# RWKV solver in a hybrid encoder: single 128x1024 stream transposes, and a chain bank given to the attention

## The chip, the cores and the metric

One core of a Trainium2 chip. The metric is the device time of one execution in microseconds, the median of several runs. Engine names in the profile: PE is TensorE's matmuls, PEld its weight loads, DVE VectorE, ACT ScalarE, POOL GpSimd, SP SyncE.

## The reference

Two layers over x of 512 tokens by 1024 channels. Each layer computes

```
h  = RMSNorm(x);  P = h @ W_in
yA = bidirectional Mamba-2 SSD          (8 heads of 64)
yB = bidirectional RWKV-7 time mix      (8 heads of 64) * silu(gate)
yC = differential attention             (4 heads, two softmax maps each) * silu(gate)
yD = grouped-query attention            (4 query heads of 128, 2 key heads) * silu(gate)
x  = x + RMSNorm(concat(yA, yB, yC, yD) @ W_out)
```

The part that matters here is the RWKV scan, for each head and each direction a state S of 64x64 over 512 steps:

```
sa  = S a_t
S   = S * w_t + outer(sa, b_t) + outer(v_t, k_t)      a = -kk, b = kk * a
y_t = S r_t
```

## The kernel before

All is float32. The large projections split each weight and each activation into a high and a low float32r part and take three products; the low part of a weight is made on GpSimd from ScalarE's high part (L144, L145). A plain float32 product is two instructions on TensorE in the trace.

**RWKV.** `rwkv` goes over four pairs of heads, j = 0 to 3 (L522). The scan is done in eight chunks of 64 steps. For each pair, both heads (e), both directions (d) and all chunks (pairs cp, halves p) are worked at once: 32 blocks of 64x64. In a chunk, steps that depend on one another form a triangular system, and its inverse is needed. The solver (L537 to L599) inverts the 16x16 diagonal blocks on VectorE, 15 steps of two small operations each (L556 to L563), with the four blocks of a chunk along the partitions and the 32 systems side by side, and then builds the 64x64 inverse from them by three rounds of block products `ph` (L589 to L598).

To bring the diagonal blocks into that layout and back, the kernel uses VectorE's transposes of 32x32 blocks and ScalarE's copies:

- L548 to L551: four ScalarE copies of 32 partitions each gather the quarter blocks on the diagonal of `ba` (the tile AT0) into half of DT; one transpose of 128x512; one multiply-add under the mask `th` picks the right 16 columns into As2.
- L565 to L576: two scalings by `th` make Dx; a transpose of 128x512 and four copies fill DN (the inverse blocks); a second transpose and eight copies fill DT (their transposes). DN and DT were set to zero by GpSimd before.

Then follow the groups of 32 small products, each into two PSUM banks, one for each head e: `pm` (L582), `ph`, `px` (L604), `pu` (L611), `pw` (L616), `pq` (L621, L623), `pp` (L636), `py` (L647). In pm and px the output goes to `half[p ^ e]`: for the second head, the block of partitions 0 to 63 is written to 64 to 127, and the other way round. The copies of A (L466 to L469) and the reads in pu and pw follow that swap. `ph` writes to `half[p]`, without a swap. Last comes the chain over the chunks (L659 to L676): for each chunk and direction a product `bk` and one VectorE operation for the next state.

**PSUM.** Eight banks: two `pj` for projections, two `g` for all else in RWKV, one `ga` for the attention (scores, transposed probabilities `ptp`, outputs `ob`, transposed q and k `pqt`), and for the RWKV part `ch0`, `ch1` and `yb`. `G2` names the pair g, g, `C2` the pair ch0, ch1.

**The order of the work.** `fill` hands out pieces of the attention and of the projections between the solver's steps, as many microseconds' worth as constants such as F_SV, F_MG and F_CH say; `ahead` hands out the next pair's preparation. That makes the program's order. A planner then makes each engine's fixed order from it: the earliest in program order goes first, and what waits for a bank or a result may be passed by later work.

Of the kernel before, what the change touches and what calls it, by code (L numbers as in the profile page):

```python
# [10 lines left out]
F32 = mybir.dt.float32  # L11
F32R = mybir.dt.float32r
AF = mybir.ActivationFunctionType
ALU = mybir.AluOpType
# [40 lines left out]
C_TH = C_NOM + 64  # L55
C_I64 = C_TH + 2
C_N = C_I64 + 64

# [17 lines left out]
def trunk(ctx: ExitStack, tc: tile.TileContext, x_in, win, wwd, wdt, wout, w2a, cols, rows, sscal, consts, out, dbg=None,  # L76
# [4 lines left out]
    def mm(o, lhsT, rhs, start, stop, skip=False):  # L81
        PE.matmul(o, lhsT, rhs, start=start, stop=stop, skip_group_check=skip)  # L82
# [27 lines left out]
    id64 = cst[:, C_I64:C_I64 + 64]  # L110
    th = [cst[:, C_TH + n:C_TH + n + 1] for n in range(2)]
    nhalf = cst[:, C_NHALF:C_NHALF + 16]
# [140 lines left out]
    def rwkv(i, lay, pw, ps, rp, fill):  # L253
# [162 lines left out]
        half = [slice(0, 64), slice(64, 128)]  # L416
        quad = [(slice(32 * q, 32 * q + 32), slice(32 * (q % 2), 32 * (q % 2) + 32)) for q in range(4)]

# [5 lines left out]
        def banks(tags, shape, nm):  # L424
            return [ps.tile(shape, F32, tag=t, name=nm) for t in tags]

        G2, C2 = ("g", "g"), ("ch0", "ch1")
        zeros = cr[:, 272:273].to_broadcast([128, 128])
# [19 lines left out]
        def turned(src, nm):  # L448

            pt = ps.tile([128, 4, 128], F32, tag="g", name=nm)  # L450
            for cp in range(4):
                PE.transpose(pt[:, cp, :], src[:, cp * 128:cp * 128 + 128], ident)
            return pt.rearrange("p c (e k) -> p e c k", e=2)
# [3 lines left out]
        def by_tokens(j):  # L457

            s = sts[j]
            yield from products(j, 1)  # L460
            s["KT"], s["A"] = tokens("KT", "kt"), tokens("A", "ta")
            for d in range(2):
                S.activation(VT[:, :, d], turned(s["v"][d], "pv5"), AF.Copy)
                S.activation(s["KT"][:, :, d], turned(chans(s["BK"][d][:, 1]), "pk5"), AF.Copy)
                yield
                pt = turned(chans(s["a"][:, d]), "pa5")  # L466
                S.activation(s["A"][:, 0, d], pt[:, 0], AF.Copy)
                for p in range(2):
                    S.activation(s["A"][half[1 - p], 1, d], pt[half[p], 1], AF.Copy)  # L469
                yield  # L470
# [51 lines left out]
        for j in range(4):  # L522
# [13 lines left out]

            unit = lambda t, q: t[quad[q][0], :, :, :, quad[q][1]].rearrange("p e d c (h t) -> p t h (e d c)", h=2)  # L537
            thu = lambda t, q: t[quad[q][0]].rearrange("p (t h u) -> p t h u", t=16, h=2)
            sv = rp.tile([128, 1024], F32, tag="sv", name="sv", bufs=1)
            As = sv[:, 0:512].rearrange("p (t s) -> p t s", t=16)  # L540
            As2 = sv[:, 512:768].rearrange("p (t s) -> p t s", t=16)
            Ti = sv[:, 768:1024].rearrange("p (t s) -> p t s", t=16)
            DT, DN = tokens("DT", "dt"), tokens("DN", "dn")
            close = DT[:, 0].rearrange("p d c t -> p (d c t)")
            G.memset(DN, 0.0)
            G.memset(sv[:, 768:1024], 0.0)
            G.memset(sv[:, 768:1024:17], 1.0)
            for q in range(4):  # L548
                S.activation(thu(close, q), unit(ba, q), AF.Copy)
            V.transpose(out=sv[:, 0:512], in_=close)  # L550
            V.scalar_tensor_tensor(As2, As[:, :, 0:16], th[0], As[:, :, 16:32], op0=ALU.mult, op1=ALU.add)  # L551
            G.memset(DT, 0.0)

            bam = AT[0].rearrange("p e d c a t -> p (e d c) a t")[:, :, 0, :]
            G.tensor_tensor(bam, bam, nomask.unsqueeze(1).to_broadcast([128, 16, 64]), op=ALU.mult)
# [8 lines left out]

            Dx = sv[:, 0:512].rearrange("p (t h s) -> p t h s", t=16, h=2)  # L565
            for h in range(2):
                V.tensor_scalar(Dx[:, :, h, :], Ti, th[h], None, op0=ALU.mult)
            close = sv[:, 512:1024]
            V.transpose(out=close.rearrange("p (t h s) -> p t h s", t=16, h=2), in_=Dx.rearrange("p t h s -> p s h t"))
            for q in range(4):  # L570
                S.activation(unit(DN, q), thu(close, q), AF.Copy)
            V.transpose(out=close, in_=sv[:, 0:512])
            for q in range(4):
                for e in range(2):
                    S.activation(unit(DT, (q + 2 * e) % 4)[:, :, :, 8 * e:8 * e + 8], thu(close, q)[:, :, :, 8 * e:8 * e + 8],
                                 AF.Copy)  # L576
            step(1, F_MG)
# [3 lines left out]
            for d, cp, e, p in every:  # L581
                mm(pm[e][half[p ^ e], 4 * d + cp, :], ba[half[p], e, d, cp, :], DN[half[p], e, d, cp, :], True, True)  # L582
            S.activation(flat(Mp[:, 0]), pm[0], AF.Copy)
# [19 lines left out]
            for d, cp, e, p in every:  # L603
                mm(px[e][half[p ^ e], 4 * d + cp, :], ka[half[p], e, d, cp, :], VT[half[p], e, d, cp, :], True, True)  # L604
            S.activation(flat(X0[:, 0]), px[0], AF.Copy)
# [4 lines left out]
            for d, cp, e, p in every:  # L610
                mm(pu[e][half[p], 4 * d + cp, :], TT[half[p ^ e], e, d, cp, :], X0[half[p ^ e], e, d, cp, :], True, True)  # L611
            S.activation(flat(U0[:, 0]), pu[0], AF.Copy)
            V.tensor_copy(flat(U0[:, 1]), pu[1])
            pw = banks(G2, [128, 8, 64], "pw")
            for d, cp, e, p in every:
                mm(pw[e][half[p], 4 * d + cp, :], TT[half[p ^ e], e, d, cp, :], A[half[p ^ e], e, d, cp, :], True, True)  # L616
            step(1, F_MG)
# [6 lines left out]
            for p in range(2):  # L624
                V.tensor_tensor(Q[:, :, p::2], pq[p].rearrange("p (d c) v -> p d c v", d=2),
                                lamC[:, :, p::2].unsqueeze(3).to_broadcast([128, 2, 4, 64]), op=ALU.mult)
            W = tokens("W", "kt")
            S.activation(flat(W[:, 0]), pw[0], AF.Copy)
# [30 lines left out]
            for cc in range(1, 8):  # L659
                if cc == C_LAG:  # L660
                    ahead.finish()
                    if j < 3:
                        ahead.gens = [products(j + 1, 0)]
                Sn = [None, None]
                for d in range(2):
                    if cc < 7:
                        bk = ps.tile([128, 8, 64], F32, tag=f"ch{d}", name=f"bk{d}")
                        for e in range(2):
                            mm(bk[half[e], 0, :], P[half[e], d, cc, :], St[d][half[e]], True, True)
                        Sn[d] = rp.tile([128, 64], F32, tag=f"S{d}", name=f"S{d}", bufs=2)  # L670
                        V.scalar_tensor_tensor(Sn[d], bk[:, 0, :], lamC[:, d, cc:cc + 1], Q[:, d, cc, :],
                                               op0=ALU.mult, op1=ALU.add)
                    for e in range(2):
                        mm(yb[half[e], rev(d, cc)], St[d][half[e]], R[half[e], d, cc, ::1 - 2 * d], False, True, True)
                St = Sn
                step(2, F_CH)  # L676
# [241 lines left out]
    def pT_av(p, va, qb, ps, ap):  # L918

        pt = ps.tile([128, 4, 128], F32, tag="g", name="ptp")  # L920
        for kt in range(4):
            PE.transpose(pt[:, kt, :], p[:, kt * 128:kt * 128 + 128], ident)
        ptS = ap.tile([128, 4, 128], F32, tag="ptS", name="ptS", bufs=1)
        S.activation(ptS, pt, AF.Copy)
        ob = ps.tile([128, 128], F32, tag="g", name="ob")
        for kt in range(4):
            mm(ob, ptS[:, kt, :], va[:, kt, :], kt == 0, kt == 3)
        return ob
# [252 lines left out]
    ps = Bank(psc, {"pj": 2, "g": 2, "ga": 1})  # L1181
    pa = Bank(psc, ps.bufs, {"g": "ga"})
    hT["hi"] = hpool.tile([128, 8, L], F32R, tag="hhi", name="hhi")
# [9 lines left out]
    for i in range(depth):  # L1193
# [9 lines left out]
        with tc.tile_pool(name="psr", bufs=1, space=PSUM, reuse_waits="tile") as psr, \  # L1203
                tc.tile_pool(name="rw", bufs=1, reuse_waits="tile") as rp:
            rwkv(i, lay, pw, Bank(psc, ps.bufs, {}, Bank(psr, {"ch0": 1, "ch1": 1, "yb": 1})), rp, fill)

# [131 lines left out]
def _consts():  # L1338
# [11 lines left out]
    c[:, C_NOM:C_NOM + 64] = (s[:, None] // 16 < np.arange(64)[None, :] // 16)  # L1350
    for n in range(2):
        c[:, C_TH + n] = (p % 32 // 16 == n)
    c[:, C_I64:C_I64 + 64] = (s[:, None] == np.arange(64)[None, :])
# [104 lines left out]
```

## Time and profile before

| | us |
|---|---|
| median of 3 runs (1862.32 to 1870.21) | 1866.43 |
| the profiled execution | 1859.53 |
| its span, first to last instruction | 1857.7 |
| TensorE matmuls busy | 1600.4 (86%) |
| VectorE busy | 1031.5 (56%) |
| ScalarE busy | 937.2 (50%) |
| GpSimd busy | 694.7 (37%) |

The mean granted clock of TensorE is 0.927 of full speed. The span is what lies between the first and the last instruction; the execution's own time is a little longer. Busy time counts an engine's instructions without its waits; matmuls overlap, so their busy time is that of their union. A group's row gives the busy time, the mean of one in ns, and behind the second bar the idle time of the engine before it and what ended it.

### The profile page before, as it was taken

Reading aid. Unit: us, or ns where it says so; the run is one execution under the profiler, and the core shown is the slowest. Engines: PE = TensorE matmul, PEld = TensorE weight load, DVE = VectorE, ACT = ScalarE, POOL = GpSimd, SP = SyncE. Lnnn points to the kernel's source line nnn. Section 1 sums busy time; section 2 is a strip of 40 time slices with the busy share of each in tenths; the row PEclk is TensorE's granted clock in tenths of the full one; section 3 lists DMA queues with packets and bytes.
Section 4 is the critical chain, followed back from the end, with each engine's and each line's share of the span. In section 5 each row is a group of like instructions: output and inputs, shape, how many; then the busy total and the mean of one; then the engine's idle time right before and its main releaser. Section 6 shows DMA issues by size and latency. Waiting matters only on the chain. (4 is left out here: it accounts for less than half of the span.)

```text
span 1857.7 us, 36925 instructions
## 1 busy us (share of the span) xinstructions
PE 1600.4 (86%) x15200; PEld 1305.4 (70%) x15200; DVE 1031.5 (56%) x2098; ACT 937.2 (50%) x1750; POOL 694.7 (37%) x712
## 2 busy tenths in 40 slices
PE   6888987987888898988897999889689888999888
PEld 6567766766766777866785777676577666777666
DVE  4565465654573436886246554646455724378852
ACT  4657365457437245443346663744664472454431
POOL 4443233323152225444444333233332422355343
PEclk9889988989989899999999798989898898999999
DMA  4111101111011014222421010011110110141223
GB/s 151 61 40 39 36 26 44 44 35 41 25 35 52 30 41 147 70 70 91 136 99 51 33 42 30 29 48 43 35 46 19 35 52 25 52 138 57 91 82 117
DMA packets 57513, 108.50 MB, mean 58 GB/s; under 512 B 6784, under 2 KB 8704, under 8 KB 57344
## 3 DMA queue, kind: packets, MB, share of 16 engines
q1 hardware_dynamic: 57344, 106.14, 17.2%
q8 instruction: 119, 1.95, 0.4%
q14 instruction: 50, 0.41, 0.1%
HBM read 95.63 MB, written 10.49 MB: 57 GB/s over the span
## 5 line engine op out<-in xcount | busy, mean ns | idle before, releaser
L145 POOL TENSOR_TENSOR wlo<-wf,whi 128x512 fp32r<-128x512 f32 x228 | 316.9, 1396 | 510.2 <-ACT whi L144 475.6
L82 PE MATMUL pjt<-whi,hhi 128*128 128x256 f32 x960 | 297.0, 309 | 10.6 <-ACT raw L270 9.5
L82 PE MATMUL pjt<-wlo,hhi 128*128 128x256 f32 x960 | 290.9, 303 | 1.8 <-POOL wlo L145 1.8
L82 PE MATMUL pjt<-whi,hlo 128*128 128x256 f32 x960 | 288.7, 301 | 0.0
L144 ACT ACTIVATE whi<-wf 128x512 fp32r<-128x512 f32 x228 | 141.7, 629 | 199.6 <-PE pjt L82 91.5
L82 PEld LDWEIGHTS pjt<-whi,hhi 128*128 128x128 f32 x960 | 194.8, 203 | 26.7 <-ACT raw L270 10.6
L82 PEld LDWEIGHTS pjt<-whi,hlo 128*128 128x128 f32 x960 | 194.7, 203 | 9.1 <-issue 7.4
L82 PEld LDWEIGHTS pjt<-wlo,hhi 128*128 128x128 f32 x960 | 194.5, 203 | 9.0 <-issue 6.0
L82 PE MATMUL pjc<-hhi,whi 128*128 128x512 f32 x384 | 159.4, 416 | 9.3 <-ACT raw L270 5.2
L82 PE MATMUL pjc<-hlo,whi 128*128 128x512 f32 x384 | 157.1, 409 | 0.0
L82 PE MATMUL pjc<-hhi,wlo 128*128 128x512 f32 x384 | 156.4, 409 | 0.0
L900 ACT ACTIVATE p<-sc,nm 128x512 f32<-128x512 f32 x96 | 65.8, 685 | 124.9 <-DVE nm L897 113.4
L897 DVE TENSOR_REDUCE nm<-sc 128x1 f32<-128x512 f32 x96 | 65.9, 687 | 107.5 <-PE sc L82 106.6
L82 PE MATMUL sc<-qT,qT 64*128 64x512 f32 (+1 forms) x256 | 103.2, 502 | 20.5 <-DVE qT L938 7.2
L82 PE MATMUL mix<-whi,ylo 128*128 128x512 f32 x256 | 106.3, 415 | 5.4 <-DVE ylo L1241 5.4
L82 PE MATMUL mix<-wlo,yhi 128*128 128x512 f32 x256 | 104.4, 408 | 0.0
L82 PE MATMUL mix<-whi,yhi 128*128 128x512 f32 x256 | 99.6, 411 | 2.0 <-ACT yhi L1240 2.0
L82 PEld LDWEIGHTS pjc<-hhi,whi 128*128 128x128 f32 x384 | 75.7, 197 | 30.8 <-ACT raw L270 6.0
L82 PEld LDWEIGHTS pjc<-hhi,wlo 128*128 128x128 f32 x384 | 75.4, 196 | 19.5 <-issue 3.0
L1248 ACT ACTIVATE whi<-wf 128x512 fp32r<-128x512 f32 x64 | 40.5, 632 | 94.4 <-PE mix L82 59.4
L82 PEld LDWEIGHTS pjc<-hlo,whi 128*128 128x128 f32 x384 | 75.4, 196 | 16.7 <-issue 2.2
L1249 POOL TENSOR_TENSOR wlo<-wf,whi 128x512 fp32r<-128x512 f32 x32 | 44.4, 1391 | 105.8 <-ACT whi L1248 101.1
(349 smaller groups left out, 3681.4 us busy)
## 6 DMA issues: line engine op xcount, KB each, us to landing
wf<-in_win_dram SPq DMA_DIRECT2D x224, 256.0 KB, 3.0
wf<-in_wout_dram SPq DMA_DIRECT2D x64, 256.0 KB, 2.7
y<-y_dram SPq DMA_DIRECT2D x24, 256.0 KB, 3.3
xt<-in_x_dram SPq DMA_DIRECT2D x8, 512.0 KB, 4.3
y_dram<-y SPq DMA_DIRECT2D x16, 256.0 KB, 2.7
y_dram<-rs SPq DMA_DIRECT2D x8, 256.0 KB, 2.0
x_dram<-t SPq DMA_DIRECT2D x8, 256.0 KB, 2.3
xt<-x_dram SPq DMA_DIRECT2D x4, 512.0 KB, 3.8
```

What stands on the lines that cost most here:

```text
L82: PE.matmul(o, lhsT, rhs, start=start, stop=stop, skip_group_check=skip)
L144: S.activation(hi, wf, AF.Copy)
L145: G.tensor_tensor(lo, wf, hi.bitcast(F32), op=ALU.subtract)
L897: V.tensor_reduce(nm, sc, axis=AX, op=ALU.max, negate=True)
L900: S.activation(p, sc, AF.Exp, bias=nm, accum_out=sm)
L1248: S.activation(hi, wf, AF.Copy)
L1249: (V if kt % 2 else G).tensor_tensor(lo, wf, hi.bitcast(F32), op=ALU.subtract)
```

## The change

The transposes work on whole tiles of 128x1024 and carry the off-diagonal quarter blocks along; masks (`at`, seven columns of constants instead of two) pick what is wanted. The copies and the memsets of DN and DT are gone, and so is the swap of partition halves in A, pm, px, pu and pw. pw is issued behind pq. The attention's transposed probabilities and outputs use a bank `gb` during RWKV (in the rest of the layer `ga` as before); `C2` is now `ch` and one of the two g banks, and the chain's second direction uses g.

```diff
-    th = [cst[:, C_TH + n:C_TH + n + 1] for n in range(2)]
+    at = [cst[:, C_TH + n:C_TH + n + 1] for n in range(7)]
...
-        G2, C2 = ("g", "g"), ("ch0", "ch1")
+        G2, C2 = ("g", "g"), ("ch", "g")
...
-                pt = turned(chans(s["a"][:, d]), "pa5")
-                S.activation(s["A"][:, 0, d], pt[:, 0], AF.Copy)
-                for p in range(2):
-                    S.activation(s["A"][half[1 - p], 1, d], pt[half[p], 1], AF.Copy)
+                S.activation(s["A"][:, :, d], turned(chans(s["a"][:, d]), "pa5"), AF.Copy)
...
-            sv = rp.tile([128, 1024], F32, tag="sv", name="sv", bufs=1)
-            As = sv[:, 0:512].rearrange("p (t s) -> p t s", t=16)
+            sv = rp.tile([128, 1536], F32, tag="sv", name="sv", bufs=1)
+            As = sv[:, 0:1024].rearrange("p (t h s) -> p t h s", t=16, h=2)
...
-            G.memset(DN, 0.0)
...
-            for q in range(4):
-                S.activation(thu(close, q), unit(ba, q), AF.Copy)
-            V.transpose(out=sv[:, 0:512], in_=close)
-            V.scalar_tensor_tensor(As2, As[:, :, 0:16], th[0], As[:, :, 16:32], op0=ALU.mult, op1=ALU.add)
-            G.memset(DT, 0.0)
+            blocks = lambda t: t.rearrange("p u (q t) -> p t q u", q=4)
+            whole = lambda t: t.rearrange("p e d c t -> p (e d c) t")
...
+            V.transpose(out=sv[:, 0:1024].rearrange("p (t q u) -> p t q u", t=16, q=4), in_=blocks(bam))
+            V.scalar_tensor_tensor(As2, As[:, :, 0, 0:16], at[0], As[:, :, 0, 16:32], op0=ALU.mult, op1=ALU.add)
+            V.scalar_tensor_tensor(As2, As[:, :, 1, 0:16], at[1], As2, op0=ALU.mult, op1=ALU.add)
+            V.scalar_tensor_tensor(As2, As[:, :, 1, 16:32], at[2], As2, op0=ALU.mult, op1=ALU.add)
...
-            for h in range(2):
-                V.tensor_scalar(Dx[:, :, h, :], Ti, th[h], None, op0=ALU.mult)
-            close = sv[:, 512:1024]
-            V.transpose(out=close.rearrange("p (t h s) -> p t h s", t=16, h=2), in_=Dx.rearrange("p t h s -> p s h t"))
             for q in range(4):
-                S.activation(unit(DN, q), thu(close, q), AF.Copy)
-            V.transpose(out=close, in_=sv[:, 0:512])
-            for q in range(4):
-                for e in range(2):
-                    S.activation(unit(DT, (q + 2 * e) % 4)[:, :, :, 8 * e:8 * e + 8], thu(close, q)[:, :, :, 8 * e:8 * e + 8],
-                                 AF.Copy)
+                V.tensor_scalar(Dx[:, :, q, :], Ti, at[3 + q], None, op0=ALU.mult)
+            V.transpose(out=blocks(whole(DN)), in_=Dx.rearrange("p t q s -> p s q t"))
+            V.transpose(out=blocks(whole(DT)), in_=Dx)
...
-                mm(pm[e][half[p ^ e], 4 * d + cp, :], ba[half[p], e, d, cp, :], DN[half[p], e, d, cp, :], True, True)
+                mm(pm[e][half[p], 4 * d + cp, :], ba[half[p], e, d, cp, :], DN[half[p], e, d, cp, :], True, True)
...
-                        bk = ps.tile([128, 8, 64], F32, tag=f"ch{d}", name=f"bk{d}")
+                        bk = ps.tile([128, 8, 64], F32, tag="g" if d else "ch", name=f"bk{d}")
...
-        pt = ps.tile([128, 4, 128], F32, tag="g", name="ptp")
+        pt = ps.tile([128, 4, 128], F32, tag="h", name="ptp")
...
-        ob = ps.tile([128, 128], F32, tag="g", name="ob")
+        ob = ps.tile([128, 128], F32, tag="h", name="ob")
...
-            rwkv(i, lay, pw, Bank(psc, ps.bufs, {}, Bank(psr, {"ch0": 1, "ch1": 1, "yb": 1})), rp, fill)
+            pa.names["h"], pa.other = "gb", Bank(psr, {"gb": 1})
+            rwkv(i, lay, pw, Bank(psc, ps.bufs, {}, Bank(psr, {"ch": 1, "yb": 1})), rp, fill)
+            pa.names["h"] = "ga"
```

px loses its swap like pm, and pu and pw read `half[p]` of TT, X0 and A. The lines of pw stand behind the evacuation of pq into Q, ahead of the copies into W.

## Rows read from the trace of the kernel before

**Rows 1.** Stretches: length, busy PE, PEld, DVE, ACT, POOL, PEclk, DMA share, GB/s
```profile
110.00:680.00 570.00, 487.11 (x5987) 398.89 (x5988) 305.61 (x673) 306.03 (x572) 185.02 (x180) 0.92 0.11 36
1033.00:1604.00 571.00, 491.30 (x5991) 402.12 (x5991) 305.67 (x673) 306.52 (x574) 185.18 (x180) 0.91 0.11 36
...
420.70:427.30 6.60, 3.54 (x13) 2.94 (x14) 0.29 (x1) 6.41 (x13) 5.33 (x5) 0.50 0.17 59
```

**Rows 2.** TensorE's waits, stretch 110 to 680: total us, times, longest
```profile
PE ptp L922 <- DVE p L1057: 7.7, 7, 2.4
...
PE ptp L922 <- ACT p L900: 5.9, 5, 2.7
...
PE pv L82 <- ACT bh L284: 5.1, 2, 4.6
...
PE sc L82 <- ACT p L900: 2.6, 3, 1.1
...
PE pjt L82 <- ACT raw L270: 2.0, 1, 2.0
PE sc L82 <- ACT y L1059: 1.9, 2, 1.6
PE sc L82 <- ACT y L1080: 1.7, 1, 1.7
...
PE ptp L922 <- ACT KT L464: 1.4, 1, 1.4
...
PE pqt L933 <- ACT y L1059: 1.3, 1, 1.3
```

**Rows 3.** Groups of instructions: ScalarE's copies around the solver, both layers
```profile
L575 ACT ACTIVATE DT<-sv 32x256 f32<-32x256 f32 x64 | 41.8, 652 | 0.7
...
L571 ACT ACTIVATE DN<-sv 32x512 f32<-32x512 f32 x32 | 35.5, 1109 | 6.0 <-DVE sv L569 5.3
L549 ACT ACTIVATE DT<-AT 32x512 f32<-32x512 f32 x32 | 35.3, 1102 | 7.6 <-DVE AT L444 7.3
...
L469 ACT ACTIVATE A<-pa 64x256 f32<-64x256 f32 x32 | 12.1, 380 | 0.4
```

**Rows 4.** ScalarE in order of time, in the third solver: start, length
```profile
414.81 5.30 ACT L575 ACTIVATE DT<-sv 32x256 f32<-32x256 f32 x8
...
422.53 0.63 ACT L284 ACTIVATE bh<-sqc 128x512 fp32r<-128x512 f32 x1
```

**Rows 5.** Small products on TensorE: two runs in time, then groups
```profile
318.94 2.08 PE L82 MATMUL ph<-DN,Mp 64*64 64x64 f32 x64
...
324.48 1.16 PE L82 MATMUL px<-VT,AT 64*64 64x64 f32 x64
...
L82 PE MATMUL ph<-DN,Mp 64*64 64x64 f32 x1024 | 37.9, 227 | 12.9 <-DVE DN L597 12.9
...
L82 PE MATMUL pu<-X,DN 64*64 64x64 f32 x512 | 17.7, 261 | 8.5 <-DVE X L606 6.6 <-ACT X L605 1.9
...
L82 PE MATMUL pm<-DN,AT 64*64 64x64 f32 x512 | 16.5, 224 | 0.0
...
L82 PE MATMUL px<-VT,AT 64*64 64x64 f32 x512 | 13.5, 222 | 0.0
...
L82 PE MATMUL pw<-A,DN 64*64 64x64 f32 x512 | 12.9, 246 | 0.0
```

**Rows 6.** VectorE's groups around the solver; L551 by source line: min/median/max
```profile
L569 DVE STREAM_TRANSPOSE sv<-sv 128x512 f32<-128x512 f32 x8 | 8.9, 1111 | 0.1
...
L572 DVE STREAM_TRANSPOSE sv<-sv 128x512 f32<-128x512 f32 x8 | 5.7, 711 | 5.9 <-ACT DN L571 5.9
...
L551 DVE SCALAR_TENSOR_TENSOR sv<-sv,cst x8: 867/1988/2012, 116.2 to 1470.9; 128x256 f32<-128x256 f32 x8
```

**Rows 7.** VectorE's evacuations of pq and pp
```profile
L639 DVE TENSOR_TENSOR P<-pp,cst 128x256 f32<-128x256 f32 x32 | 13.3, 415 | 4.8 <-PE pp L82 4.3
...
L625 DVE TENSOR_TENSOR Q<-pq,lamC 128x512 f32<-128x512 f32 x16 | 10.3, 684 | 3.9 <-PE pq L82 3.9
```

More of the change, by code (lines that the diff above doesn't have):

```diff
@@ L55 @@
 C_TH = C_NOM + 64
-C_I64 = C_TH + 2
+C_I64 = C_TH + 7
 C_N = C_I64 + 64
@@ L416, in rwkv @@
         half = [slice(0, 64), slice(64, 128)]
-        quad = [(slice(32 * q, 32 * q + 32), slice(32 * (q % 2), 32 * (q % 2) + 32)) for q in range(4)]
         each = [(cp, e, p) for cp in range(4) for e in range(2) for p in range(2)]
@@ L534, in step @@
                 fill(us)
-            unit = lambda t, q: t[quad[q][0], :, :, :, quad[q][1]].rearrange("p e d c (h t) -> p t h (e d c)", h=2)
-            thu = lambda t, q: t[quad[q][0]].rearrange("p (t h u) -> p t h u", t=16, h=2)
-            sv = rp.tile([128, 1024], F32, tag="sv", name="sv", bufs=1)
-            As = sv[:, 0:512].rearrange("p (t s) -> p t s", t=16)
-            As2 = sv[:, 512:768].rearrange("p (t s) -> p t s", t=16)
-            Ti = sv[:, 768:1024].rearrange("p (t s) -> p t s", t=16)
-            DT, DN = tokens("DT", "dt"), tokens("DN", "dn")
-            close = DT[:, 0].rearrange("p d c t -> p (d c t)")
-            G.memset(DN, 0.0)
-            G.memset(sv[:, 768:1024], 0.0)
-            G.memset(sv[:, 768:1024:17], 1.0)
-            for q in range(4):
-                S.activation(thu(close, q), unit(ba, q), AF.Copy)
-            V.transpose(out=sv[:, 0:512], in_=close)
-            V.scalar_tensor_tensor(As2, As[:, :, 0:16], th[0], As[:, :, 16:32], op0=ALU.mult, op1=ALU.add)
-            G.memset(DT, 0.0)
+            sv = rp.tile([128, 1536], F32, tag="sv", name="sv", bufs=1)
+            As = sv[:, 0:1024].rearrange("p (t h s) -> p t h s", t=16, h=2)
+            As2 = sv[:, 1024:1280].rearrange("p (t s) -> p t s", t=16)
+            Ti = sv[:, 1280:1536].rearrange("p (t s) -> p t s", t=16)
+            DT, DN = tokens("DT", "dt"), tokens("DN", "dn")
+            G.memset(sv[:, 1280:1536], 0.0)
+            G.memset(sv[:, 1280:1536:17], 1.0)
+            blocks = lambda t: t.rearrange("p u (q t) -> p t q u", q=4)
+            whole = lambda t: t.rearrange("p e d c t -> p (e d c) t")
             bam = AT[0].rearrange("p e d c a t -> p (e d c) a t")[:, :, 0, :]
+            V.transpose(out=sv[:, 0:1024].rearrange("p (t q u) -> p t q u", t=16, q=4), in_=blocks(bam))
+            V.scalar_tensor_tensor(As2, As[:, :, 0, 0:16], at[0], As[:, :, 0, 16:32], op0=ALU.mult, op1=ALU.add)
+            V.scalar_tensor_tensor(As2, As[:, :, 1, 0:16], at[1], As2, op0=ALU.mult, op1=ALU.add)
+            V.scalar_tensor_tensor(As2, As[:, :, 1, 16:32], at[2], As2, op0=ALU.mult, op1=ALU.add)
             G.tensor_tensor(bam, bam, nomask.unsqueeze(1).to_broadcast([128, 16, 64]), op=ALU.mult)
@@ L563, in rwkv @@
                 V.tensor_tensor(Ti[:, jj + 1:16, 0:jj + 1], Ti[:, jj + 1:16, 0:jj + 1], o3, op=ALU.add)
-            Dx = sv[:, 0:512].rearrange("p (t h s) -> p t h s", t=16, h=2)
-            for h in range(2):
-                V.tensor_scalar(Dx[:, :, h, :], Ti, th[h], None, op0=ALU.mult)
-            close = sv[:, 512:1024]
-            V.transpose(out=close.rearrange("p (t h s) -> p t h s", t=16, h=2), in_=Dx.rearrange("p t h s -> p s h t"))
-            for q in range(4):
-                S.activation(unit(DN, q), thu(close, q), AF.Copy)
-            V.transpose(out=close, in_=sv[:, 0:512])
-            for q in range(4):
-                for e in range(2):
-                    S.activation(unit(DT, (q + 2 * e) % 4)[:, :, :, 8 * e:8 * e + 8], thu(close, q)[:, :, :, 8 * e:8 * e + 8],
-                                 AF.Copy)
+            Dx = sv[:, 0:1024].rearrange("p (t q s) -> p t q s", t=16, q=4)
+            for q in range(4):
+                V.tensor_scalar(Dx[:, :, q, :], Ti, at[3 + q], None, op0=ALU.mult)
+            V.transpose(out=blocks(whole(DN)), in_=Dx.rearrange("p t q s -> p s q t"))
+            V.transpose(out=blocks(whole(DT)), in_=Dx)
             step(1, F_MG)
@@ L603, in rwkv @@
             for d, cp, e, p in every:
-                mm(px[e][half[p ^ e], 4 * d + cp, :], ka[half[p], e, d, cp, :], VT[half[p], e, d, cp, :], True, True)
+                mm(px[e][half[p], 4 * d + cp, :], ka[half[p], e, d, cp, :], VT[half[p], e, d, cp, :], True, True)
             S.activation(flat(X0[:, 0]), px[0], AF.Copy)
@@ L610, in rwkv @@
             for d, cp, e, p in every:
-                mm(pu[e][half[p], 4 * d + cp, :], TT[half[p ^ e], e, d, cp, :], X0[half[p ^ e], e, d, cp, :], True, True)
+                mm(pu[e][half[p], 4 * d + cp, :], TT[half[p], e, d, cp, :], X0[half[p], e, d, cp, :], True, True)
             S.activation(flat(U0[:, 0]), pu[0], AF.Copy)
             V.tensor_copy(flat(U0[:, 1]), pu[1])
-            pw = banks(G2, [128, 8, 64], "pw")
-            for d, cp, e, p in every:
-                mm(pw[e][half[p], 4 * d + cp, :], TT[half[p ^ e], e, d, cp, :], A[half[p ^ e], e, d, cp, :], True, True)
             step(1, F_MG)
@@ L626, in rwkv @@
                                 lamC[:, :, p::2].unsqueeze(3).to_broadcast([128, 2, 4, 64]), op=ALU.mult)
+            pw = banks(G2, [128, 8, 64], "pw")
+            for d, cp, e, p in every:
+                mm(pw[e][half[p], 4 * d + cp, :], TT[half[p], e, d, cp, :], A[half[p], e, d, cp, :], True, True)
             W = tokens("W", "kt")
@@ L1181, in trunk @@
     ps = Bank(psc, {"pj": 2, "g": 2, "ga": 1})
-    pa = Bank(psc, ps.bufs, {"g": "ga"})
+    pa = Bank(psc, ps.bufs, {"g": "ga", "h": "ga"})
     hT["hi"] = hpool.tile([128, 8, L], F32R, tag="hhi", name="hhi")
@@ L1350, in _consts @@
     c[:, C_NOM:C_NOM + 64] = (s[:, None] // 16 < np.arange(64)[None, :] // 16)
-    for n in range(2):
-        c[:, C_TH + n] = (p % 32 // 16 == n)
+    b16 = s // 16
+    for n, m in enumerate((b16 % 2 == 0, b16 == 2, b16 >= 2, b16 == 0, b16 == 1, b16 == 2, b16 == 3)):
+        c[:, C_TH + n] = m
     c[:, C_I64:C_I64 + 64] = (s[:, None] == np.arange(64)[None, :])
```

## The prediction

> **What bounds the kernel now.** I read the table by stretches first, then TensorE's waits by cause, then the groups of instructions, then a few stretches in order of time. The two stretches in which the solver runs (the RWKV part of each layer) hold 1141 of the 1857.7 us. In each TensorE is busy 487 to 491 of some 570 us, while VectorE and ScalarE stand at 306 and GpSimd at 185 [rows 1]: TensorE sets the pace, and no other engine is near its own limit. It idles 82.9 us in the first and 79.7 in the second, 162.6 together, and it was granted 0.92 and 0.91 of its clock, so 45.6 + 51.4 = 97 us of full-speed work are lost beside: 0.6 us for each idle one. From within one wait of 4.6 us on, the granted clock was 0.50, the lower of the two levels, for 6.6 us [rows 1]. The change can gain in three ways: TensorE waits less, keeps the higher level more, or issues less. The list of waits shows that no single one rules: the kinds that bear on the change are 1.3 to 7.7 us a stretch each, and they end on VectorE and ScalarE in turn [rows 2]. The second layer's stretch is the first's over again (571 us, 491.3 busy), so I work with the first and double.
>
> **ScalarE's copies.** Each of the eight solvers loses 4 + 4 + 8 copies. They are 35.3 + 35.5 + 41.8 = 112.6 us in all [rows 3], 14 a solver. The copies of A go from three to one in each direction: two of 0.38 us, with a third of that width, become one twice as wide, between 0.38 and 0.76, so 6 to 12 us more. Two GpSimd memsets a solver go as well; GpSimd waits for others most of the time, and they count as nothing. ScalarE is not the bound, so its 120 us are not 120 us of the span. What counts are TensorE's waits for a ScalarE result that stood behind these copies. The clearest: eight copies into DT run for 5.30 us, and only behind them the norm's bh at 422.53 [rows 4]. TensorE waits 4.6 us for that bh (the longest of "pv from bh") [rows 2]. Of the waits of the transposed probabilities for p (5.9, the longest 2.7) I take 4.0: the longest and one of 1.3 lie in the fourth solver among its DN and DT copies. Of "raw" 2.0, of the wait behind KT 1.4, and of the scores waiting for p 1.1, its longest. That is 4.6 + 4.0 + 2.0 + 1.4 + 1.1 = 13.1 a layer, **26** in both. Bounds: 0, where the next late result stands right behind, and these rows in full in both layers, 34.
>
> The chain itself (copies, transpose, copies) also gets shorter, but the product that needs DN, pm, waited 0.0 [rows 5]: filler from the projections hides it, so I count nothing. If that cover were gone, the chain's 4 + 4 + 8 copies a solver would be worth up to 14 us each. The first half gains little in any case: four copies of 1.10, a transpose of 0.71 and one multiply-add of up to 1.99 are 7.1 us; in their place come a transpose of twice the size and three multiply-adds.
>
> **VectorE's added work.** A transpose of 128x512 takes 0.71 plain and 1.11 with a strided read [rows 6]. The three of 128x1024 have a strided read, a strided read and write, and a strided write. A strided write is not in the trace; I price it like the read and add 0.4 for each half: 2.2 + 3.0 + 2.2 = 7.4 against 2.5 before, so 4.9 more (bounds 1.7, all plain, and 6.5, all strided on both sides). Two more multiply-adds, 0.87 to 1.99 each; I take the low end, since one of the three meets GpSimd's masking as the one before did: 1.7. Two more scalings of 128x256, priced like P's evacuation of that width, 0.415 [rows 7]: 0.8. Together 7.4 a solver, 59 us for eight (bounds 34 and 90). VectorE idles nearly half the time, so most of it lies beside TensorE. What is queued behind the new lump of some 7 us on VectorE is the softmax maximum and the masks of the next products, for which TensorE waits. I charge it by TensorE's idle share of the stretch, 82.9 / 570 = 0.145: **+9** (bounds 0 and 59).
>
> **Four groups of small products.** Before, pm, px, pu and pw write to the swapped half of the partitions for e = 1, so four quarters of the array take turns; after, every one writes to its own half, so two quarters do. The trace has both patterns: ph runs in two quarters already. 64 instructions of ph took 2.08 us, 64 of px 1.16 [rows 5]. By group means, 64 instructions of ph take 37.9/16 = 2.37, of pu 2.21, pm 2.06, px 1.69 and pw 1.61 (the slower ones were issued half by half, because one bank was late, and so in two quarters already). At ph's pace the four cost 9.48 instead of 7.57: 1.91 a solver, **+15** for eight, in TensorE's own time, which nothing hides. Bounds: 0, and 32 groups of 0.92 (2.08 less 1.16), 29.
>
> The Trainium skill has a rule that speaks to this (TensorE: Matmul & The Clock Gate, Part 3: Packing small matmuls, The mechanism): a weight load overlaps running matmuls only when its row group differs. The row halves take turns before and after alike, so by the rule alone these groups would keep their time and the term would be 0; ph against px in the same stretch contradicts it.
>
> **The banks.** The attention's transposed probabilities and outputs get a bank of their own. The waits that end on the release of the shared one are the scores after an output y (1.9 and 1.7) and the transposed q and k after y (1.3) [rows 2]: 4.9 a layer, **10** for both. Bounds: 0, and 20, should as much again come loose.
>
> The solver pays with a bank: five pairs now draw their second bank from the two that everything else in RWKV uses. pw is issued behind pq, and its second bank is that which Q's evacuation has to free: two of 0.684. The second direction of pp needs the bank that P and R of the first direction read, 0.415 and about as much for R. That of py needs Y0's copy, a copy of P's width, 0.4 [rows 7]. That is 1.37 + 0.83 + 0.4 = 2.6 us a solver of possible standstill. Behind the waiting product on TensorE stand the next filler products, which need none of these banks, and the order within an engine is made by a planner that can take them first. I take half: **+10** for eight. Bounds: 0, and twice the 2.6 (VectorE is busy half the time and may come late), 42. ph's second bank changes nothing, since the next round needs the same sum. In the chain, bk of the second direction now takes turns with the next head pair's preparation; the filler that the program puts into each step (F_CH) covers it, and without that each of 48 steps would wait for one evacuation of some 0.7.
>
> **The sum.** Waits that go: 26 + 10 = 36. With each idle microsecond 0.6 of full-speed work is lost; a lower level also has causes that stay, so I add half, 0.3: 11, together 47. Costs: 15 + 10 + 9 = 34. Net -13: the profiled execution's 1859.5 becomes 1846.5. It lies 6.9 below the median of the runs shown (1866.4), so the forecast is **1853**, 0.7% faster.
>
> **The rivals.**
> - *The shared banks decide (slower).* Without the bank term the net is -23. With p us of standstill a solver and 0.3 of lost clock on it, the cost is 8 x 1.3 x p = 10.4 p; it passes the gain at p = 2.3 and ends over 0.5% slower from p = 3.1. At p = 4 it is +18: 1884; at 5.2 it is 1897. For it: pw stands right behind pq with no filler between, and every solver has three such places. Against: the planner's reordering, seen where groups are split over other work.
> - *The gain is taken up again (no change).* TensorE waits for VectorE as often as for ScalarE; with ScalarE's copies gone, the next late VectorE result ends the same pause. Half of the 47 goes, 23.5; of the costs the 9 is then the same thing, so 25 stay: +2, 1868.
> - *Two quarters run as fast as four,* since the row halves take turns in both: -28, 1838. Against it stands ph. By the rule of the Trainium skill named above (TensorE: Matmul & The Clock Gate, The mechanism) it would be so.
> - *The attention comes loose.* With a second bank scores are issued ahead, and p is ready when its transposes come up: the rest of those waits, 1.9 and the 7.7 for VectorE's p, go too. 9.6 x 2 x 1.3 = 25: -38, 1828. For it: TensorE needs the same bank for scores, transposes and outputs now. Against: within one query block the steps still follow one another.
>
> **How the numbers follow.** Forecast 0.42 (its own range 1840 to 1862), shared banks 0.17, taken up again 0.22, two quarters as fast 0.06, attention loose 0.13. Below 0.5%, 9.3 us, nothing can be told from no change: faster is under 1857.1, slower over 1875.8. Faster: 0.30 of the forecast, 0.06 and 0.13, so 0.49. Same: 0.12 of the forecast and 0.17 of "taken up again", 0.29. Slower: 0.17 and the last 0.05, 0.22. The range reaches into the loose attention and into the shared banks up to p = 4: 1818 to 1886.
>
> **What would show it.** In the profile after: ScalarE's busy time some 120 us less and VectorE's 34 to 90 more; px, pm, pu and pw at 2.1 to 2.4 us for 64; pv's wait for bh under 1 us, and no score waiting for y. Idle time of the two stretches at 125 to 150 us would fit the forecast. Right against it would be waits of pw for Q, or of pp for R, over 2 us a solver (shared banks), or a wait for ScalarE that only changed its name to VectorE (taken up again). It is wrong if the four groups keep their time, if the granted clock falls in the solver, or if the time leaves the range.

## Result and the profile after

The kernel after takes **1846.07 us** (median; 1844.03 to 1847.89), the kernel before on the same chip 1868.32: ratio 0.9883, 95% interval 0.9851 to 0.9914. The profiled execution is 1844.0 us with a span of 1842.1; that of before was 1859.5. So -15.5 by the profiles and -22 by the medians, where -13 was forecast; the profiled execution of before lies 8.8 below the median of its four runs.

The two solver stretches of after, in the table by stretches (columns as in [rows 1]):

```profile
110.00:671.00 561.00, 504.55 (x6013) 417.35 (x6007) 332.97 (x689) 246.90 (x493) 182.83 (x173) 0.92 0.11 37
1027.00:1586.00 559.00, 504.33 (x5990) 417.08 (x5988) 332.88 (x689) 246.84 (x493) 182.88 (x173) 0.92 0.11 37
```

Beside [rows 1] they are 9 and 12 us shorter. TensorE's idle time fell from 162.6 to 56.5 + 54.7 = 111.2, by 51; but its busy time in them rose by 17.4 + 13.0 = 30. More than half of what was won as idle time was paid back as busy time; the rows of the four groups below grew by 25 us. ScalarE went from 306 to 247 a stretch, VectorE from 306 to 333. Outside these stretches the program became 5 us longer.

TensorE's waits in the first of them (total, times, longest):

```profile
PE sc L82 <- ACT p L886: 7.1, 3, 4.4
...
PE pw L82 <- DVE Q L608: 4.5, 2, 2.3
PE ptp L908 <- ACT p L886: 3.7, 3, 2.1
PE p L82 <- ACT bh L284: 3.2, 1, 3.2
...
PE ptp L908 <- DVE p L1043: 3.0, 5, 1.6
```

Against [rows 2]: pv's wait for bh is gone, and no score waits for y. But p, another product that reads bh, waits 3.2 for it where it waited 0.3 (over the kernel 12.4 where it waited 7.2), so a part of that wait only moved. The transposed probabilities wait 3.7 + 3.0 where they waited 5.9 + 7.7. New is pw's wait for Q, and the scores wait longer for p (2.6 before).

The four groups of small products, and pq, which kept its four quarters. First runs of 64 in order of time, in one solver (start, length), then the groups over the kernel:

```profile
312.20 2.08 PE L82 MATMUL px<-VT,AT 64*64 64x64 f32 x64
317.28 2.08 PE L82 MATMUL pu<-X,DN 64*64 64x64 f32 x64
321.04 1.16 PE L82 MATMUL pq<-VT,KT 64*64 64x64 f32 x64
```
```profile
L82 PE MATMUL pm<-DN,AT 64*64 64x64 f32 x512 | 23.0, 241 | 0.0
L82 PE MATMUL pw<-A,DN 64*64 64x64 f32 x512 | 22.8, 246 | 8.8 <-DVE Q L608 8.2 <-issue 0.6
L82 PE MATMUL pu<-X,DN 64*64 64x64 f32 x512 | 20.5, 235 | 6.5 <-DVE X L592 6.3
L82 PE MATMUL px<-VT,AT 64*64 64x64 f32 x512 | 19.4, 230 | 3.3 <-DVE DN L583 3.3
```

They were 16.5, 12.9, 17.7 and 13.5 [rows 5]: 60.6 became 85.7. By group means that is 2.4 to 2.9 us for 64, where the forecast looked for 2.1 to 2.4. VectorE's new instructions (the three transposes, the scalings, the multiply-adds):

```profile
L544 DVE SCALAR_TENSOR_TENSOR sv<-sv,cst 128x256 f32<-128x256 f32 x8 | 19.2, 2398 | 0.1
L561 DVE STREAM_TRANSPOSE DN<-sv 128x1024 f32<-128x1024 f32 x8 | 19.0, 2373 | 0.3
L543 DVE STREAM_TRANSPOSE sv<-AT 128x1024 f32<-128x1024 f32 x8 | 15.8, 1980 | 0.2
L562 DVE STREAM_TRANSPOSE DT<-sv 128x1024 f32<-128x1024 f32 x8 | 15.8, 1978 | 0.0
L560 DVE TENSOR_SCALAR sv<-sv,cst 128x256 f32<-128x256 f32 x32 | 11.4, 413 | 0.1
L545 DVE SCALAR_TENSOR_TENSOR sv<-sv,cst 128x256 f32<-128x256 f32 x8 | 7.4, 928 | 0.1
L546 DVE SCALAR_TENSOR_TENSOR sv<-sv,cst 128x256 f32<-128x256 f32 x8 | 3.7, 468 | 0.1
```

VectorE's busy time over the kernel rose from 1031.5 to 1085.0 (+53.5; 59 forecast), ScalarE's fell from 937.2 to 817.5 (120, as forecast).

### The profile page after: what moved, and what is told of

The parts are those of the page before. It is cut to its first block, busy times and chain, and to the rows that moved or that the text cites. A ratio compares the mean times of both kernels' runs of the same rounds, so it can differ in the third digit from the quotient of the medians.

```text
span 1842.1 us, 36771 instructions
## 1 busy us (share of the span) xinstructions
PE 1637.3 (89%) x15200; PEld 1343.2 (73%) x15200; DVE 1085.0 (59%) x2130; ACT 817.5 (44%) x1590; POOL 689.1 (37%) x696
## 5 line engine op out<-in xcount | busy, mean ns | idle before, releaser
L145 POOL TENSOR_TENSOR wlo<-wf,whi 128x512 fp32r<-128x512 f32 x228 | 325.2, 1430 | 507.4 <-ACT whi L144 472.7
L82 PE MATMUL sc<-qT,qT 64*128 64x512 f32 (+1 forms) x256 | 103.2, 498 | 16.5 <-ACT p L886 14.2
L82 PEld LDWEIGHTS pjc<-hhi,wlo 128*128 128x128 f32 x384 | 74.3, 193 | 20.2 <-issue 2.6
L1237 POOL TENSOR_TENSOR wlo<-wf,whi 128x512 fp32r<-128x512 f32 x32 | 44.4, 1390 | 108.1 <-ACT whi L1236 103.5
```

Of the source, the lines that this page charges most:

```text
L145: G.tensor_tensor(lo, wf, hi.bitcast(F32), op=ALU.subtract)
L1237: (V if kt % 2 else G).tensor_tensor(lo, wf, hi.bitcast(F32), op=ALU.subtract)
```

## Experiments

The theory was the prediction's own sum: the copies' waits pay for two quarters and VectorE's work, and bank against bank comes to nothing. Ratios are to the kernel before on the same chip, with 95% intervals.

**t_only: the transposes with the banks of before.**
```diff
-        G2, C2 = ("g", "g"), ("ch", "g")
+        G2, C2 = ("g", "g"), ("ch0", "ch1")
...
-            pa.names["h"], pa.other = "gb", Bank(psr, {"gb": 1})
...
```


> The transpose part alone, with the banks of before (pw still behind pq). Both parts pay: ScalarE loses its 112 us of copies, waits of TensorE behind them go (30 to 40 us), the two-quarter products cost 15 to 25; 1848 to 1862 us, ratio 0.990 to 0.997, scores and transposed probabilities still wait for the shared attention bank. Rival, the bank alone made the gain: 1866 to 1885, for the two-quarter products and VectorE's 53 us are then pure cost. Rival, the transposes alone made it: 1840 to 1848.

1843.44 us, ratio 0.9871 (0.9849 to 0.9894): the rival, the transposes alone made the gain, and the theory that both parts pay fell. TensorE's idle time over the kernel (span less busy time) fell from 257.3 to 235.5, and its busy time is that of before (1603.6 against 1600.4), although two quarters are paid in it; the granted clock was 0.937 against 0.927. Of the waits in the traces, those that ended on ScalarE fell from 88.8 to 73.5 us, those on VectorE stayed (147.0 and 144.8).

**b_only: before, with the banks of after** (and pw behind Q, as there).
```diff
-        G2, C2 = ("g", "g"), ("ch0", "ch1")
+        G2, C2 = ("g", "g"), ("ch", "g")
...
```


> The bank part alone (the second attention bank, the solver on the shared ring, pw behind pq), with the copies and the swapped halves of before. Both parts pay: ptp's waits of 35.5 us fall below 20, the ring costs 10 to 25; 1850 to 1866 us. Rival, the bank alone made the gain: 1840 to 1850. Rival, the transposes alone made it: 1866 to 1885.

1861.92 us, 0.9969 (0.9948 to 0.9990): 6 us of gain alone, and the waits ahead of ptp fell from 35.5 to 19.2, as expected. Whether the parts add can't be told: 0.9871 x 0.9969 = 0.984, and the whole change gave 0.9883, a difference at the edge of the intervals.

**ring_only: after, with the attention on one bank again.**
```diff
-            pa.names["h"], pa.other = "gb", Bank(psr, {"gb": 1})
...
-            pa.names["h"] = "ga"
```


> The kernel after with the attention back on one bank, and the bank that was taken for it left unused: the solver pays for sharing its two banks, the attention gets nothing. The new transposes with the banks of before took 1843.4, the kernel after 1846.1. Theory (the sharing costs some 10 us and the attention's second bank gives back about as much): 1850 to 1862. Rival A (sharing costs nothing and the second bank gives nothing): 1841 to 1848. Rival B (sharing costs over 2 us a solver, and the bank gives back nearly all): over 1862.

1845.76 us, 0.9882 (0.9864 to 0.9901): rival A. Against t_only the shared banks cost 2 us, and against after the attention's second bank gives 0, both within the measurement. The groups of pp, pw and py over the kernel show what happens beneath, first t_only:

```profile
L82 PE MATMUL pp<-AT,W 64*64 64x128 f32 x512 | 20.2, 276 | 1.6 <-DVE W L615 1.6
L82 PE MATMUL pw<-A,DN 64*64 64x64 f32 x512 | 19.4, 230 | 0.6 <-issue 0.6
L82 PE MATMUL py<-AT,VT 64*64 64x64 f32 x512 | 16.0, 248 | 6.2 <-DVE R L627 6.2
```
then ring_only:
```profile
L82 PE MATMUL pp<-AT,W 64*64 64x128 f32 x512 | 26.9, 282 | 0.3 <-DVE R L627 0.3
L82 PE MATMUL pw<-A,DN 64*64 64x64 f32 x512 | 21.9, 240 | 8.8 <-DVE Q L608 7.8 <-issue 0.9
L82 PE MATMUL py<-AT,VT 64*64 64x64 f32 x512 | 19.5, 224 | 1.4 <-DVE rs L888 0.7 <-DVE R L627 0.4
```
and after:
```profile
L82 PE MATMUL pp<-AT,W 64*64 64x128 f32 x512 | 32.5, 320 | 0.6 <-DVE R L627 0.6
L82 PE MATMUL py<-AT,VT 64*64 64x64 f32 x512 | 22.7, 248 | 0.8 <-DVE R L627 0.4
```

pp hardly waits for R. Its rows grow instead, 20.2, 26.9, 32.5 us: near 190 us its 64 instructions of one solver stand in four separate runs in after (4, 24, 20 and 16), in two in t_only (26 and 38), with scores and projections between. That the late bank splits them is argued from the program; no run isolates it, and the rows of a group that alternates with others overlap theirs. TensorE's whole idle time falls in the same order, 235.5, 225.3, 204.8, its busy time rises, 1603.6, 1625.5, 1637.3, and the time stays. The granted clock falls too, 0.937, 0.931, 0.924 in these three executions: one minus the clock, times the span, is 116, 128 and 140 us. So most of the 34 us of busy time between t_only and after may be the lower clock, and only the rest the split products. It is not the one execution: ring_only's four runs were granted 0.931 to 0.937, after's four 0.924 to 0.926, and both take the same time. What the attention's second bank gains in idle time is lost in the clock; why the clock fell, no run shows.

**before_two: before, with two quarters** (the halves are then not where the next step looks for them; only the time is read).
```diff
-                mm(px[e][half[p ^ e], 4 * d + cp, :], ka[half[p], e, d, cp, :], VT[half[p], e, d, cp, :], True, True)
+                mm(px[e][half[p], 4 * d + cp, :], ka[half[p], e, d, cp, :], VT[half[p], e, d, cp, :], True, True)
```
(pm, pu and pw alike.)

> The kernel before with the four groups written and read without the swap of halves (the data of the second head then do not fit, only the time is read): 64 instructions of each at ph's pace, +15 to +25 us: 1880 to 1893. Rival, it costs nothing: 1862 to 1873.

1878.71 us, 1.0056 (1.0035 to 1.0076): **+10.4**, just under the range:

```profile
L82 PE MATMUL pw<-A,DN 64*64 64x64 f32 x512 | 19.5, 233 | 0.0
L82 PE MATMUL px<-VT,AT 64*64 64x64 f32 x512 | 18.8, 221 | 0.0
```

px goes from 13.5 to 18.8, pw from 12.9 to 19.5, near to after, so two quarters are not as fast as four. Set beside that of before, this trace has every instruction of ScalarE, VectorE and GpSimd in the same order, and all but 67 of TensorE's 15200 (counted here and below as the fewest that would have to be moved); what changed here is the quarters alone.

**quads: after, with the swapped halves back** in the four groups; VectorE's evacuations undo the swap.
```diff
-            V.tensor_copy(flat(X0[:, 1]), px[1])
+            for p in range(2):
+                V.tensor_copy(flat(X0[half[p], 1]), px[1][half[1 - p]])
```


> The changed kernel with the swapped halves back in the four groups, so that four quarters take turns; the swap is undone in VectorE's evacuation (two copies of half the partitions for one of all). Two quarters cost TensorE's own time: px, pm, pu and pw fall from 85.7 to some 60 us busy, 15 to 25 us less: 1821 to 1834. Rival, two quarters cost nothing since other pauses take the difference up: 1843 to 1855, with VectorE's 32 additional copies on top.

1837.56 us, 0.9846 (0.9814 to 0.9878): 8.5 less than after, between the two expectations; the intervals of the two ratios overlap, so the size is rough. The four groups fell from 85.7 to 72.7, not to some 60: pw stayed at 21.6. It pays 32 more VectorE instructions (busy 1107.9 against 1085.0).

**before_nocopy: before without the copies into DN and DT** (lines 571 and 575; the blocks of the inverse stay zero).
```diff
-                S.activation(unit(DN, q), thu(close, q), AF.Copy)
...
-                    S.activation(unit(DT, (q + 2 * e) % 4)[:, :, :, 8 * e:8 * e + 8], thu(close, q)[:, :, :, 8 * e:8 * e + 8],
-                                 AF.Copy)
```


> The kernel before without ScalarE's 4 + 8 copies into DN and DT (77 us of ScalarE's time); the blocks of the inverse stay zero, so the products that use them work on zeros, with the same instructions. Theory (the copies cost through ScalarE's queue and through the chain behind them; this is most of what the new transposes bring, and two quarters and VectorE's added work are paid out of it): 1836 to 1852, that is 16 to 32 us less than before, with TensorE's idle time in the two solver stretches down from 162 to 140 or less. Rival (the copies lie beside other work and the gain comes from elsewhere, the copies of A or the first four copies): 1856 to 1870.

1824.16 us, 0.9765 (0.9740 to 0.9789): **-44**, more than either theory (29 by the profiled executions; this one was the slowest of its six). Summed over TensorE's waits by the engine that ended them, those of ScalarE fell from 88.8 to 56.0 us and those of VectorE stayed (147.0 and 147.2). Among its waits over the whole kernel:

```profile
PE ptp L916 <- ACT p L894: 8.6, 11, 1.5
...
PE p L82 <- ACT bh L284: 7.5, 6, 2.6
...
PE pjt L82 <- ACT raw L270: 3.1, 3, 1.3
...
PE sc L82 <- ACT y L1053: 1.6, 2, 0.8
```

and in before:

```profile
PE ptp L922 <- ACT p L900: 15.1, 14, 2.7
...
PE pv L82 <- ACT bh L284: 10.2, 4, 4.6
...
PE pjt L82 <- ACT raw L270: 9.5, 4, 3.3
...
PE p L82 <- ACT bh L284: 7.2, 6, 2.7
...
PE sc L82 <- ACT y L1059: 3.7, 4, 1.6
PE sc L82 <- ACT y L1080: 3.4, 2, 1.7
```

pv's wait for bh is gone altogether. So the scores' waits for y, which I had put down to the shared bank, were for the most part a late ScalarE. In the first stretch of before, y at 581.57 us stands right behind two DT copies of 1.26 us, and the scores wait 1.7 for it; the y at 171.70, for which they wait 1.6, stands behind other work of ScalarE.

The planner made a new order here: the copies aside, 112 of ScalarE's 1654 instructions and 578 of TensorE's 15200 stand in another place than in before. The 44 us are the queue without the copies and this order together.

**t_copies: t_only with 12 idle copies on ScalarE.**
```diff
+            for q in range(4):
+                S.activation(junk[32 * q:32 * q + 32], sv[32 * q:32 * q + 32, 0:512], AF.Copy)
+            for q in range(8):
+                S.activation(junk[32 * (q % 4):32 * (q % 4) + 32, 0:256], sv[32 * (q % 4):32 * (q % 4) + 32, 0:256], AF.Copy)
```


> The new transposes with the banks of before, and 12 copies of the old sizes put back on ScalarE behind the last transpose, into a buffer that nothing reads: ScalarE's queue has its 77 us again, but no product waits for these copies. The same without them took 1843.4. Theory (what counts is what stands behind the copies in ScalarE's queue): back up by 10 to 25 us, 1853 to 1868, with the wait for the norm's bh back at some 4 us a layer. Rival (what counts is the chain of copies in front of the next product): no change, 1840 to 1848.

1856.43 us, 0.9941 (0.9926 to 0.9957): 13 back, as the theory had it. p's wait for bh rose from 13.2 to 23.8 us over the kernel, 5 a layer, but all waits that ended on ScalarE together did not (73.5 and 72.0; VectorE's rose from 144.8 to 150.9). The copies were shorter than meant, since they read and write plain rows:

```profile
L567 ACT ACTIVATE junk<-sv 32x256 f32<-32x256 f32 x64 | 26.5, 414 | 1.4
L565 ACT ACTIVATE junk<-sv 32x512 f32<-32x512 f32 x32 | 20.0, 626 | 6.2 <-DVE sv L560 5.6
```

46.5 us of queue, not 77. From this I concluded that of the 44 some 30 had to be the chain of copies in front of pm, or the zeros. Four kernels on that:

**before_zero: the copies stay, the data are zeros** (the inverse's blocks are scaled by zero).
```diff
-                V.tensor_scalar(Dx[:, :, h, :], Ti, th[h], None, op0=ALU.mult)
+                V.tensor_scalar(Dx[:, :, h, :], Ti, zero, None, op0=ALU.mult)
```


> The kernel before with the inverse's scaling by zero in place of the mask: every copy and transpose stays, only the blocks of the inverse are zeros and with them the data of many products. It separates the data from the copies in the 44 us that the kernel without the 4 + 8 copies gained. Theory (the data doesn't matter): 1858 to 1872, as before. Rival (zeros keep the clock up and are much of the 44): 1828 to 1850.

1870.01 us, 1.0000 (0.9980 to 1.0020): the data cost nothing.

**before_junk: the copies go where nothing reads them** (the inverse's blocks are zeros).
```diff
-                S.activation(unit(DN, q), thu(close, q), AF.Copy)
+                S.activation(unit(junk, q), thu(close, q), AF.Copy)
```
(The copies into DT alike.)

> The kernel before with the 4 + 8 copies written to a buffer that nothing reads, in place of DN and DT, whose blocks stay zero: ScalarE's queue and VectorE's are as long as before, but no product waits for the copies. Without these copies it took 1824.2, with them 1867.8. Theory (the queue costs 13, as 12 idle copies did in the new kernel, and the chain copies, transpose, copies in front of pm some 30): 1832 to 1843. Rival (the queue is nearly all, and the idle copies in the new kernel met a looser schedule): 1850 to 1866.

1868.99 us, 1.0001 (0.9983 to 1.0019), above both ranges. My theory of the chain fell. The copies are as long as in [rows 3], and the waits nearly as in before:

```profile
L576 ACT ACTIVATE junk<-sv 32x256 f32<-32x256 f32 x64 | 41.9, 655 | 0.7
L572 ACT ACTIVATE junk<-sv 32x512 f32<-32x512 f32 x32 | 35.5, 1109 | 5.7 <-DVE sv L570 5.0
```
```profile
PE ptp L923 <- ACT p L901: 13.5, 12, 2.7
...
PE pv L82 <- ACT bh L284: 9.7, 3, 4.6
PE pjt L82 <- ACT raw L270: 8.6, 4, 2.5
```

No product waits for the copies here, and the time is that of before. So is the order: all of ScalarE's, VectorE's and GpSimd's instructions, and all but 14 of TensorE's, stand where they stood (before_zero likewise). Take the copies away, and 44 us go, but with a new order. How much the copies' time in the queue would give in the order of before, no run here shows.

**before_apart: VectorE's second transpose no longer waits for the copies into DN.**
```diff
-            sv = rp.tile([128, 1024], F32, tag="sv", name="sv", bufs=1)
+            sv = rp.tile([128, 1536], F32, tag="sv", name="sv", bufs=1)
...
+            close = sv[:, 1024:1536]
             V.transpose(out=close, in_=sv[:, 0:512])
```


> The kernel before with a third piece of buffer for the second transpose of the inverse, so that VectorE no longer waits there for the four copies into DN; all copies stay. The trace of before has that wait at 5.9 us of VectorE's idle time in eight solvers, once with the softmax's work behind it. Without the copies the kernel took 44 us less, with them in a buffer that nothing reads 0. Theory (ScalarE's own queue is what costs, 77 us of copies and what stands behind them): 1860 to 1872, as before. Rival (VectorE's standstill behind the copies is much of the 44): 1835 to 1855.

1872.85 us, 1.0023 (1.0008 to 1.0039): nothing gained, rather 4.7 lost, just over the range. VectorE's standstill (5.9 us of idle time in [rows 6]), taken alone, was not the cost. No work was added here; the planner moved 50 of ScalarE's and 324 of TensorE's instructions. So a new order may be worth several microseconds by itself, and differences of that size between kernels of different order are to be read with that in mind.

**t_free: t_only, its last two transposes into a buffer that nothing reads** (the inverse's blocks are zeros).
```diff
-            V.transpose(out=blocks(whole(DT)), in_=Dx)
+            V.transpose(out=blocks(whole(junk)), in_=Dx)
```
(DN alike.)

> The new transposes with the banks of before, the last two transposes written to a buffer that nothing reads, so that no product waits for them; the inverse's blocks are zeros, set by GpSimd. VectorE's work is the same. With the chain this took 1843.4. It tells what the chain still costs after the change. Theory (the chain's copies were what cost; what is left of it, two scalings and two transposes of some 7 us a solver, is partly hidden): 1828 to 1840. Rival A (nothing is left of the chain): 1841 to 1847. Rival B (the chain costs as much as ever, and the transposes only took out the queue): under 1828.

1845.78 us, 0.9872 (0.9847 to 0.9898), as t_only: rival A. No cost of the chain is seen after the change either.

**t_quads: t_only with four quarters, pw ahead of pq.**
```diff
-                mm(pw[e][half[p], 4 * d + cp, :], TT[half[p], e, d, cp, :], A[half[p], e, d, cp, :], True, True)
+                mm(pw[e][half[p ^ e], 4 * d + cp, :], TT[half[p], e, d, cp, :], A[half[p], e, d, cp, :], True, True)
...
-            V.tensor_copy(flat(W[:, 1]), pw[1])
+            for p in range(2):
+                V.tensor_copy(flat(W[half[p], 1]), pw[1][half[1 - p]])
```


> The new transposes with the banks of before, pm, px, pu and pw back in four quarters (the swap of halves is undone by VectorE's evacuations, two of half the partitions each in place of one), and pw issued ahead of pq as before. The same transposes with two quarters took 1843.4; the kernel after gained 8.5 from four quarters. Theory (the parts are independent here: four quarters are worth 8 to 10, less some of the extra evacuations): 1830 to 1838, the fastest of all. Rival (without the second bank for the attention the gain goes into its waits): 1839 to 1846.

1835.50 us, 0.9829 (0.9812 to 0.9846): as expected, and the fastest kernel with the whole computation. Its interval lies below that of after. From quads, which has the new banks (0.9846), it can't be told apart. The place of pw changed along with the quarters, so the 7.9 us against t_only are for both.

## Why the forecast came out, step by step

The sign was right and the size near: -22 where -13 was forecast. It is luck in part that the sum came so near: the copies were worth more in before than I had charged, while the second bank and the clock, together 21 of the 47 us of gain, brought nothing in the end, and the two costs that were measured came out smaller than forecast. Two of the signs that I named also missed: the idle time of the two stretches is 111 us, under the 125 to 150, and the four groups are slower than 2.4 by their means.

- **ScalarE's copies, -26 (bounds 0 and 34): mis-sized.** Two thirds of the copies, left out of before, gave 44 us (33 of them as TensorE's waits for ScalarE). I had priced only waits with copies in plain sight ahead of them, and cut those of p to 4.0 of 5.9 a layer. Without the copies raw, p, y and most of bh come earlier. What the change itself keeps of this is less: TensorE's waits for ScalarE are 15 us lower in t_only and 24 in after, by other kinds than those I named (bh 19.9 to 12.4, the scores' wait for p 5.2 up to 14.2). That the cost is not a product's wait for these copies is shown by before_junk, in the order of before; before_zero takes out the data, before_apart VectorE's standstill. What is left is the copies' time in ScalarE's queue and the order that the planner makes without them, and these two are not separated. Why 46 us of idle copies in t_copies gave back 13 and 77 us in before gave 44, I did not settle; place, length and order differ.
- **The chain, 0: no cost seen.** pm's wait of 0.0 was to be trusted; in t_free and before_junk nothing waits for the copies or transposes, and the times don't move.
- **VectorE's added work, +9: not measured alone.** The added busy time was 53.5 for 59. From the others, if they add: t_only's -25 is -44 for the copies into DN and DT, +10 for two quarters, and 9 that remain for VectorE less whatever the first four copies and those of A gave, so 9 or more. But TensorE's waits for VectorE did not rise in t_only (144.8 from 147.0), and the orders differ; the 9 is a remainder and not a price.
- **Two quarters, +15: 10.4** by before_two; quads (8.5) and t_quads against t_only (7.9) are of that size. TensorE's busy time in the four groups rose by 22 in before_two (60.6 to 82.3), and its idle time over the kernel fell by 7 (257.3 to 250.4), so not all of it came out in the time. The spacing I took from ph is what px and pu have now. By the rule of the Trainium skill as I had applied it (TensorE: Matmul & The Clock Gate, Part 3: Packing small matmuls, The mechanism), these groups would have kept their time; px at 2.08 and pq at 1.16 in one solver of after contradict that.
- **The attention's second bank, -10, and the shared banks, +10: 0 and 2** on top of the transposes. The waits that I named for the bank went, but most of them go without the bank too: of the scores' 7.1 us for y 3.1 are left in t_only, 1.6 in before_nocopy. pw's wait for Q is 8.2 us in eight solvers, 1.0 each, between the half of 1.37 that I charged and the whole; pp's for R is nothing. What I missed is that fewer waits need not mean less time: the products of pp are issued in more pieces, and the granted clock is lower.
- **The clock, -11: there with the transposes, gone with the second bank.** By the medians of the runs, one minus the granted clock times the span is 136 to 140 us for before (four sets), 127 in t_only, 120 in ring_only and 139 in after: 11 back, and then lost. In the profiled executions, summed in steps of 4 us, it is 44.5 + 52.2 us in the solver stretches of before and 46.8 + 45.8 in after: 4 back. Between the layers, where nothing was changed, it rose from 21.1 to 27.8, and took that away; in t_only it stood at 16.8. Why it fell there is open.
- **The rivals.** "The attention comes loose" happened in the waits (idle time ahead of ptp over the kernel went from 35.5 to 12.0 us) and not in the time: TensorE's busy time took it. "Taken up again" describes the last step from t_only to after, not the change. In the rival of the shared banks, the cost passes the gain at p = 2.2 and not 2.3 (23 / 10.4).

## What to carry to other kernels

Price an engine's copies by what stands behind them in its queue too, and not only by the product that reads them: moved to a buffer that nobody reads they cost as much, removed they gave 44 us for 77 of a half-idle engine, though in a new order. Where a planner makes the order, set the orders of two traces side by side before a difference is put down to the edit: in before_apart one wait less came with a new order and 4.7 us more. A wait for a bank may be a wait for the engine that empties it; look what that engine did before. And add idle time, busy time and granted clock of the bounding engine before counting a gain: from t_only to after, 31 us less idle time came with 34 us more busy time and a clock of 0.924 in place of 0.937.

## What the hardware showed beside

- 64 instructions of 64x64 products in two quarters of the array took 1.8 times as long as 64 in four: 2.08 us against 1.16, in one solver, both at a granted clock of 1.00.
- The 128x1024 stream transpose took 1.98 us with a strided read, 1.98 with a strided write and 2.37 with both; I had estimated 2.2, 2.2 and 3.0. Writing with a stride took as long here as reading with one, and both together 0.39 more.
- The same 32x512 copy on ScalarE took 1.11 us into the solver's strided layout and 0.63 into plain rows.
